# Second MLP product of a decoder block: eight pairs of row blocks summed in PSUM, pair by pair for all four banks, weight sums and additions on VectorE

## The chip, the cores and the metric

One Trainium2 chip, of which the kernel uses one core. The metric is the device time of the program in microseconds (us), the median of several runs. The profile's times are those of one execution. PE is TensorE, DVE VectorE, ACT ScalarE, POOL GpSimd, SP SyncE, whose queue issues nearly all DMAs.

## What is computed

A decoder block for 1024 tokens of width 1024: sparse attention, sliding-window attention, gates, then an MLP of width 4096, all in float32. The change touches only the last product of the MLP and the norm behind it:

```python
h2 = rmsnorm(x, mlp_norm_w)
u = relu(h2 @ w_up)                  # [1024, 4096]
x = x + (u * u) @ w_down             # [1024, 4096] @ [4096, 1024]
return rmsnorm(x, final_norm_w)
```

## The kernel before

Float32 precision comes from splitting: `split` (line 99) makes of a 128x512 block `a` a high part `h` (a rounded copy, ScalarE, line 102) and a rest `l = a - h` (VectorE, line 107). One block product is then three matmuls, h by h, h by l and l by h (lines 1103 to 1105), each 128 by 128 weights against 512 columns.

The second product is done with Strassen's scheme (Winograd's form) of seven products in place of eight. The 32 row blocks of `w_down` (128 rows of 1024 columns) form 16 pairs; a pair has four blocks of 128x512, b11, b12 (first row block, left and right half), b21, b22. Products "1" to "7" multiply operands of the activations, which the stage before has stored ready-made in `u_d[n-1, p]`, by operands of the weights, which are b11, b21, b22 or sums of blocks. Four sums for each pair are made by `sums` (lines 1080 to 1087) on GpSimd (`"pppp"`), into four tiles `dt` of their own; the last sum equals b21 minus the second.

The loop goes over chunks of `CH = 4` pairs, and in each chunk over the products in the order 1, 2, 6, 5, 7, 3, 4 (`items`, 28 of them). For each product it takes the four token blocks `j` in turn; `chain` (line 1099) sums the four pairs of the chunk into the PSUM bank of that `j`, 12 matmuls, and the bank is then read: for products 1 and 6 by `later` (ScalarE scales it into a tile `ds`, line 1236, GpSimd adds that to the sum `x3`, line 1238), for the others by `add` (one VectorE instruction, line 1232, in the trace `x<-pdx` or `x<-pdy`). Products 1, 6, 7, 4 go on in the same four banks (group x, tiles `pdx`), 2, 5, 3 in four others (group y, `pdy`); the groups change banks from chunk to chunk.

`operands` (line 1217) loads and splits the operands of a whole product, 4 of activations (`da`, split into `dao`) and 4 of weights (`dr` or `dt`, split into `dbo`), and is called one product ahead. `dao` and `dbo` have 7 buffers each, `da` has 6, `dr` 20, `dt` 12. In the first chunk the loads are issued behind the stores of the stage before (`issue_after(stored[-2])`).

In the last chunk `norm` (line 1242) follows the additions: squares on ScalarE, a product with `gf` on GpSimd or VectorE, the scaling, and the store to `out`. The very last bank is worked in two halves of 256 columns (`pdl`).

The order of the instructions on each engine is not the order of the text: a planner simulates the program and places what is ready by its slack, and it gives the tiles their addresses by their lifetimes; a tile with `bufs=N` has at most N copies alive. Each engine then runs its list in that fixed order, and the queue of SP as well.

Of the kernel before, what the change touches and what calls it, by code (L numbers as in the profile page):

```python
# [18 lines left out]
P = 128  # L19
# [73 lines left out]
def decoder_block(tc, I, out):  # L93
# [1095 lines left out]
    wd, ops = {}, {}  # L1189

    def block(c, p, i, a):

        t = dn.tile([P, H], F32, tag="dr", name="dr", bufs=20)
        with tc.issue_after(stored[-2]) if c == 0 else nullcontext():
            nc.sync.dma_start(t, I["w_down"][2 * p + i][:, a * H:(a + 1) * H])
        return t

    def weights_down(c, which):
        for p in range(c * CH, c * CH + CH):
            if 0 in which:  # L1200
                wd[p] = {"1": block(c, p, 0, 0)}
            if 1 in which:
                wd[p]["2"] = block(c, p, 1, 0)
        for p in range(c * CH, c * CH + CH):
            if 2 in which:
                b12, wd[p]["3"] = block(c, p, 0, 1), block(c, p, 1, 1)
                t = [dn.tile([P, H], F32, tag="dt", name="dt", bufs=12) for _ in range(4)]
                sums(wd[p]["1"], b12, wd[p]["2"], wd[p]["3"], t, "pppp", True)
                wd[p].update({"4": t[3], "5": t[0], "6": t[1], "7": t[2]})
# [7 lines left out]
    def operands(c, n):  # L1217
        if c == 0 and n in "126":
            weights_down(c, {"1": (0,), "2": (1,), "6": (2,)}[n])
        elif n == "1":  # L1220
            weights_down(c, (0, 1, 2))
        for p in range(c * CH, c * CH + CH):
            a = dn.tile([P, H], F32, tag="da", name="da", bufs=6)
            with tc.issue_after(stored[-2]) if c == 0 else nullcontext():
                loads["u"] = nc.sync.dma_start(a, u_d[int(n) - 1, p]).ins
            ops[n, p] = operand(dn, a, "act", "dve", "dao", 7), operand(dn, wd[p][n], "act", "dve", "dbo", 7)
        if c == 0 and n in "1657":
            residual(*{"1": (0, 0), "6": (1, 0), "5": (1, 1), "7": (0, 1)}[n])

    def add(b, o, ps):  # L1230
        cs = slice(o * H, o * H + ps.shape[-1]) if not isinstance(o, slice) else o
        nc.vector.scalar_tensor_tensor(x3[b][:, cs], ps, r2[:, b:b + 1], x3[b][:, cs], op0=ALU.mult, op1=ALU.add)

    def later(b, o, ps):
        t = dn.tile([P, H], F32, tag="ds", name="ds", bufs=6)
        nc.scalar.activation(t, ps, AF.Copy, scale=r2[:, b:b + 1])  # L1236
        cs = slice(o * H, (o + 1) * H)
        nc.gpsimd.tensor_tensor(x3[b][:, cs], x3[b][:, cs], t, ALU.add)  # L1238

    outs = {}  # L1240

# [26 lines left out]
            nc.sync.dma_start(out[bs, cs], y[:, cs])  # L1268

    held_banks = {}  # L1270
    operands(*items[0])
    for i, (c, n) in enumerate(items):
        if i + 1 < len(items):
            operands(*items[i + 1])
        if i == 7:
            with tc.issue_after(loads["u"]):
                nc.sync.dma_start(gf, I["final_norm_w"].broadcast_to([P, D]))
        end = c == NP // CH - 1
        for j in range(4):
            first = n in "125"  # L1280
            group = ("x" if n in "1674" else "y") if c % 2 == 0 else ("y" if n in "1674" else "x")
            if first:
                held_banks[group, j] = bank(DOWN[group][j], [P, H], f"pd{group}")
            ps = held_banks[group, j]
            hi, lo = 4 + j, j
            js = slice(j * P, (j + 1) * P)
            get = lambda k, s: ops[n, c * CH + k][s]

            def product():
                chain(ps, lambda k: tuple(t[:, js] for t in get(k, 0)), lambda k: get(k, 1), first, CH)  # L1290
            last = end and n == "4" and j == 3
            if last:
                parts = [slice(H, D), slice(0, 256), slice(256, H)]
                for q in (1, 2):
                    at = parts[q]
                    ps = bank(("mm", "pt")[q % 2], [P, 256], "pdl")
                    chain(ps, lambda k: tuple(t[:, js] for t in get(k, 0)), lambda k: get(k, 1), True, CH, at)
                    add(hi, at, ps)
                    norm(hi, parts, q)
                continue  # L1300
            product()
            if n == "1":
                later(lo, 0, ps)
            elif n == "2":
                add(lo, 0, ps)
                if end:
                    norm(lo, [slice(0, H), slice(H, D)], 0)
            elif n == "6":
                later(lo, 1, ps)
            elif n == "5":  # L1310
                add(hi, 1, ps)
            elif n == "7":
                add(hi, 1, ps)
                if end and j == 3:
                    add(hi, 0, ps)
                if end:
                    norm(hi, [slice(H, D), slice(0, 256), slice(256, H)] if j == 3 else [slice(H, D), slice(0, H)], 0)
            elif n == "3":
                add(lo, 1, ps)
                if end:  # L1320
                    norm(lo, [slice(0, H), slice(H, D)], 1)
            else:
                add(hi, 0, ps)
                if end:
                    norm(hi, [slice(H, D), slice(0, H)], 1)

    for es in (dn_es, _p, _r, _d, _c):
        es.close()
# [68 lines left out]
```

## Time and profile before

| | |
|---|---|
| median of 3 runs | 1485.68 us (1485.06 to 1489.48) |
| the profiled execution, its own time | 1482.99 us |
| its span in the trace | 1481.1 us |
| PE, share of the span busy | 93% |
| DVE / ACT / POOL | 78% / 53% / 44% |
| granted TensorE clock, mean | 0.981 |
| second product, first matmul to last | 1150.02 to 1473.77 us |

The page gives busy times of engines, the span in 40 slices, the chain of work that ended last, and the costliest groups of instructions. A matmul of 512 columns is shown with 0.39 us, but matmuls are pipelined, so their pace is read from one start to the next. The PE row is therefore not a measure of lost time in a stretch; the count of matmuls in it is.

### The profile page before, as it was taken

Reading aid. Unit: us, or ns where it says so; the run is one execution under the profiler, and the core shown is the slowest. Engines: PE = TensorE matmul, PEld = TensorE weight load, DVE = VectorE, ACT = ScalarE, POOL = GpSimd, SP = SyncE. Lnnn points to the kernel's source line nnn. Section 1 sums busy time; section 2 is a strip of 40 time slices with the busy share of each in tenths; the row PEclk is TensorE's granted clock in tenths of the full one; section 3 lists DMA queues with packets and bytes.
Section 4 is the critical chain, followed back from the end, with each engine's and each line's share of the span. In section 5 each row is a group of like instructions: output and inputs, shape, how many; then the busy total and the mean of one; then the engine's idle time right before and its main releaser. Section 6 shows DMA issues by size and latency. Waiting matters only on the chain.

```text
span 1481.1 us, 21434 instructions
## 1 busy us (share of the span) xinstructions
PE 1383.5 (93%) x7084; PEld 1167.8 (79%) x7084; DVE 1150.0 (78%) x2067; ACT 787.6 (53%) x1638; POOL 657.2 (44%) x573
## 2 busy tenths in 40 slices
PE   7999997888888999987999999999999889999998
PEld 6989886677788888865878788888887768787886
DVE  8666899999988974879864676556653897979797
ACT  6335436666675475943355585555554444444455
POOL 5373865664647653589716300000000873728151
PEclk9999998999999999999999999999999999999999
DMA  8321331332322121476666364444444955453333
GB/s 266 105 76 43 87 103 50 87 82 65 81 69 66 43 58 44 121 242 213 199 180 183 115 247 160 153 147 151 157 143 154 394 197 163 132 185 95 101 101 121
DMA packets 136400, 199.26 MB, mean 135 GB/s; under 512 B 16096, under 2 KB 59232, under 8 KB 136160
## 3 DMA queue, kind: packets, MB, share of 16 engines
q1 hardware_dynamic: 136144, 197.88, 42.3%
q8 instruction: 56, 0.92, 0.3%
q14 instruction: 56, 0.46, 0.1%
q10 hardware_dynamic: 144, 0.00, 0.0%
HBM read 135.18 MB, written 55.84 MB: 129 GB/s over the span
## 4 chain that ended last, share of the span: by engine, by line
PE 52%; DVE 27%; issue 6%; DMA 6%; POOL 5%; ACT 3%; SPq 0%; DVEq 0%; ACTq 0%; POOLq 0%
DVE of_a L673 7%; PE pu L1103 7%; PE pu L1105 7%; PE pu L1104 7%; DVE dbo L107 2%; PE pdx L1105 2%; PE pdy L1104 2%; PE pdy L1105 2%; PE pdy L1103 2%; PE pdx L1104 2%; DVE wide L850 2%; PE pdx L1103 2%; PE pso L113 2%; PE pso L112 2%; PE pso L111 2%
## 5 line engine op out<-in xcount | busy, mean ns | idle before, releaser
L1083 POOL TENSOR_TENSOR dt<-dr 128x512 f32<-128x512 f32 x16 | 28.9, 1805 | 302.7 <-DMA x<-x_d 302.7
L107 DVE TENSOR_TENSOR dao<-da,dao 128x512 fp32r<-128x512 f32 x112 | 113.6, 1021 | 22.8 <-ACT dao L102 22.8
L102 ACT ACTIVATE dao<-da 128x512 fp32r<-128x512 f32 x112 | 68.6, 620 | 103.3 <-PE pdx L1105 59.2
L111 PE MATMUL mm<-of_h,of_w 128*128 128x256 f32 x416 | 121.1, 292 | 0.0
L113 PE MATMUL mm<-of_h,of_w 128*128 128x256 f32 x416 | 120.5, 291 | 0.0
L112 PE MATMUL mm<-of_h,of_w 128*128 128x256 f32 x416 | 120.3, 290 | 0.0
L853 ACT ACTIVATE wide<-wide,of_a 128x257 f32<-128x257 f32 (+9 forms) x128 | 81.0, 634 | 65.6 <-DVE of_a L850 64.8
L673 DVE TENSOR_SCALAR_CACHE_REDUCE of_a<-wide,of_a 128x768 bf16<-128x768 bf16 (+5 forms) x93 | 106.0, 1140 | 0.9
L1103 PE MATMUL pu<-XT,uo 128*128 128x512 f32 x256 | 100.0, 390 | 2.4 <-DVE u L1147 1.7
L1238 POOL TENSOR_TENSOR x<-x,ds 128x512 f32<-128x512 f32 x32 | 49.3, 1556 | 113.5 <-ACT ds L1236 113.5
L1104 PE MATMUL pu<-XT,uo 128*128 128x512 f32 x256 | 99.7, 389 | 0.0
L1105 PE MATMUL pu<-XT,uo 128*128 128x512 f32 x256 | 99.4, 389 | 0.0
L111 PE MATMUL gt<-of_h 128*128 128x512 f32 x224 | 91.2, 407 | 6.9 <-ACT of_h L333 6.9
L113 PE MATMUL gt<-of_h 128*128 128x512 f32 x224 | 91.5, 409 | 2.6 <-POOL of_h L107 2.6
L675 ACT ACTIVATE of_a<-uall,of_a 128x384 int8<-128x384 f32 (+2 forms) x93 | 66.8, 718 | 50.7 <-DVE of_a L741 30.7
L834 PE MATMUL S<-of_w 128*128 128x256 f32 (+3 forms) x320 | 79.2, 339 | 14.3 <-DVE of_a L850 14.2
L112 PE MATMUL gt<-of_h 128*128 128x512 f32 x224 | 90.8, 406 | 1.0 <-DVE of_h L334 1.0
L1105 PE MATMUL pdx<-dbo,dao 128*128 128x512 f32 x224 | 87.1, 397 | 4.6 <-DVE dao L107 4.6
L1104 PE MATMUL pdx<-dbo,dao 128*128 128x512 f32 x224 | 88.1, 396 | 2.8 <-DVE dbo L107 2.1
L1103 PE MATMUL pdx<-dbo,dao 128*128 128x512 f32 x224 | 84.4, 393 | 3.9 <-ACT dbo L102 3.9
L1104 PE MATMUL pdy<-dbo,dao 128*128 128x512 f32 x220 | 85.3, 390 | 1.1 <-DVE dbo L107 1.1
L876 PE MATMUL pt<-kept,wide 128*128 128x128 f32 x408 | 68.9, 277 | 16.8 <-DVE wide L865 7.2
(288 smaller groups left out, 4598.9 us busy)
## 6 DMA issues: line engine op xcount, KB each, us to landing
u_d<-u SPq DMA_DIRECT2D x112, 256.0 KB, 2.2
da<-u_d SPq DMA_DIRECT2D x112, 256.0 KB, 3.0
ur<-in_w_up_dram SPq DMA_DIRECT2D x32, 512.0 KB, 4.7
dr<-in_w_down_dram SPq DMA_DIRECT2D x64, 256.0 KB, 5.0
z_d<-of_g SPq DMA_DIRECT2D x32, 256.0 KB, 2.2
uall<-z_d SPq DMA_DIRECT2D x32, 256.0 KB, 3.2
raw<-in_w_out_dram SPq DMA_DIRECT2D x32, 256.0 KB, 4.3
of_g<-in_w_g_dram SPq DMA_DIRECT2D x28, 256.0 KB, 2.8
```

What stands on the lines that cost most here:

```text
L102: nc.scalar.activation(h, src, AF.Copy)
L107: (nc.gpsimd if l_on == "pool" else nc.vector).tensor_tensor(l, src, f(h), ALU.subtract)
L111: ins = nc.tensor.matmul(ps, lhsT=ah, rhs=bh, start=first, stop=False)
L112: nc.tensor.matmul(ps, lhsT=ah, rhs=bl, start=False, stop=False)
L113: nc.tensor.matmul(ps, lhsT=al, rhs=bh, start=False, stop=last)
L673: nc.vector.tensor_scalar(j, src, c, None, op0=ALU.is_lt, op1=ALU.add, accum_out=a)
L834: marks["S"] = nc.tensor.matmul(pS[:, :e - c], lhsT=st.unit(b, j), rhs=kT[:, a, k0 + c:k0 + e], start=a == 0, stop=a == 1).ins
L853: nc.scalar.activation(pe, pe, AF.Exp, bias=last, scale=-1.0, accum_out=st.sm[:, j:j + 1])
L876: nc.tensor.transpose(pt[:, k, j], prob[j0 + j][:, (a + k) * P:(a + k + 1) * P], ident)
L1103: nc.tensor.matmul(ps, lhsT=ah, rhs=xh[:, at], start=f0, stop=False, skip_group_check=True)
L1104: nc.tensor.matmul(ps, lhsT=ah, rhs=xl[:, at], start=False, stop=False, skip_group_check=True)
L1105: nc.tensor.matmul(ps, lhsT=al, rhs=xh[:, at], start=False, stop=last, skip_group_check=True)
```

## The change

The chunk has 8 pairs in place of 4, so there are two chunks and 14 products of 8 pairs. The loop now goes over `flow`, steps of (chunk, product, pair): at each step the pair's operands go through the four banks, three matmuls each, and after the last pair of a product the four banks are read one behind the other. Reading is always `add` on VectorE; `later` is gone. The weights' sums are one VectorE instruction at a step of products 2, 6, 5 and 7, three of them in place into the tiles of the blocks, one into a tile `dt` of 2 buffers; GpSimd's `sums` are gone from this stage. Loads are called 6 steps ahead and operands 4 steps ahead; `dao` and `dbo` have 9 buffers each, `dr` 32. The last product of the last chunk is done bank by bank, as before, with 8 pairs.

```diff
-    CH = 4
+    CH = 8
-    items = [(c, n) for c in range(NP // CH) for n in "1265734"]
+    flow = [(c, n, p) for c in range(NP // CH) for n in "1265734" for p in range(c * CH, c * CH + CH)]
+    def block(c, p, at):
+        wd[p, at] = dn.tile([P, H], F32, tag="dr", name="dr", bufs=32)
         with tc.issue_after(stored[-2]) if c == 0 else nullcontext():
+            nc.sync.dma_start(wd[p, at], I["w_down"][2 * p + at // 2][:, at % 2 * H:(at % 2 + 1) * H])
+    def load(c, n, p):
+        if n == "1":
+            block(c, p, 0)
+        elif n == "2":
+            for at in (1, 2, 3):
+                block(c, p, at)
+        a = da[n, p] = dn.tile([P, H], F32, tag="da", name="da", bufs=6)
+        with tc.issue_after(stored[-2]) if c == 0 else nullcontext():
+            loads["u"] = nc.sync.dma_start(a, u_d[int(n) - 1, p]).ins
...
-                sums(wd[p]["1"], b12, wd[p]["2"], wd[p]["3"], t, "pppp", True)
...
+    def operands(c, n, p):
+        b11, b12, b21, b22 = (wd.get((p, at)) for at in range(4))
+        src = {"1": b11, "2": b21, "6": b11, "5": None, "7": b12, "3": b22, "4": b21}[n]
+        if n == "2":
+            nc.vector.tensor_tensor(b12, b22, b12, ALU.subtract)
+        elif n == "6":
+            nc.vector.tensor_tensor(b11, b12, b11, ALU.add)
+        elif n == "5":
+            src = dn.tile([P, H], F32, tag="dt", name="dt", bufs=2)
+            nc.vector.tensor_tensor(src, b22, b11, ALU.subtract)
+        elif n == "7":
+            nc.vector.tensor_tensor(b21, b21, b11, ALU.subtract)
+        ops[n, p] = operand(dn, da[n, p], "act", "dve", "dao", 9), operand(dn, src, "act", "dve", "dbo", 9)
...
-    def later(b, o, ps):
-        t = dn.tile([P, H], F32, tag="ds", name="ds", bufs=6)
-        nc.scalar.activation(t, ps, AF.Copy, scale=r2[:, b:b + 1])
-        nc.gpsimd.tensor_tensor(x3[b][:, cs], x3[b][:, cs], t, ALU.add)
...
+    def products(c, n, p, j, ps=None, first=False, at=slice(None)):
+        (ah, al), x = ops[n, p]
+        js = slice(j * P, (j + 1) * P)
...
+        end = p % CH == CH - 1
+        nc.tensor.matmul(ps, lhsT=ah[:, js], rhs=x[0][:, at], start=first, stop=False, skip_group_check=True)
+        nc.tensor.matmul(ps, lhsT=ah[:, js], rhs=x[1][:, at], start=False, stop=False, skip_group_check=True)
+        nc.tensor.matmul(ps, lhsT=al[:, js], rhs=x[0][:, at], start=False, stop=end, skip_group_check=True)
+    LOAD, LEAD = 6, 4
...
+    for i, (c, n, p) in enumerate(flow):
+        end = c == NP // CH - 1
+        if i + LOAD < len(flow):
+            load(*flow[i + LOAD])
+        if i + LEAD < len(flow):
+            operands(*flow[i + LEAD])
...
+        if end and n == "4":
+            continue
         for j in range(4):
+            products(c, n, p, j)
+        if p % CH == CH - 1:
+            for j in range(4):
+                done(c, n, j)
```

## Rows read from the trace of the kernel before

**Rows 1.** The page, its first line and part 1: busy us, share, instructions
```profile
span 1481.1 us, 21434 instructions
PE 1383.5 (93%) x7084; PEld 1167.8 (79%) x7084; DVE 1150.0 (78%) x2067; ACT 787.6 (53%) x1638; POOL 657.2 (44%) x573
```

**Rows 2.** Stretches: length, busy us (x instructions) by engine, clock, DMA share, GB/s
```profile
1150.00:1160.00 10.00, 10.00 (x44) 8.05 (x43) 8.51 (x14) 7.09 (x15) 5.74 (x3) 1.00 1.05 395
...
1180.00:1190.00 10.00, 6.89 (x23) 5.04 (x22) 6.84 (x8) 4.80 (x9) 7.61 (x6) 0.83 1.05 387
...
1210.00:1220.00 10.00, 6.42 (x21) 5.24 (x22) 10.00 (x11) 3.86 (x8) 6.26 (x5) 0.83 0.52 161
...
1230.00:1240.00 10.00, 10.00 (x46) 8.26 (x44) 6.84 (x12) 3.40 (x8) 0.00 (x0) 1.00 0.72 234
...
1150.00:1473.90 323.90, 311.55 (x1357) 254.53 (x1355) 278.07 (x328) 152.68 (x294) 165.97 (x104) 0.99 0.49 161
```

**Rows 3.** Waits of PE from 1150 us on: for whom, total us, times, longest
```profile
PE pdx L1105 <- DVE dao L107: 4.6, 2, 4.1
PE pdx L1103 <- ACT dbo L102: 3.9, 2, 2.7
```

**Rows 4.** Timeline of PE around its longest wait: start us, us, operation, idle before
```profile
1213.58 1.65 PE L1105 MATMUL pdx<-dbo,dao 128*128 128x512 f32 x3 [4.08 <-DVE dao L107]
1215.03 0.63 PE L1104 MATMUL pdx<-dbo,dao 128*128 128x512 f32 x1
1215.45 0.63 PE L1105 MATMUL pdx<-dbo,dao 128*128 128x512 f32 x1
```

**Rows 5.** Timeline of PE: the stage's first matmul, 12 without a wait, its last
```profile
1150.02 0.40 PE L1103 MATMUL pdx<-dbo,dao 128*128 128x512 f32 x1
...
1440.10 0.39 PE L1103 MATMUL pdx<-dbo,dao 128*128 128x512 f32 x1
...
1440.78 0.39 PE L1103 MATMUL pdy<-dbo,dao 128*128 128x512 f32 x1
...
1442.82 0.39 PE L1103 MATMUL pdy<-dbo,dao 128*128 128x512 f32 x1
...
1473.77 0.28 PE L1105 MATMUL pdl<-dbo,dao 128*128 128x256 f32 x1
```

**Rows 6.** Groups from 1149 us on, shapes apart: count, busy us, mean ns, idle before
```profile
L107 DVE TENSOR_TENSOR dao<-da,dao 128x512 fp32r<-128x512 f32 x112 | 113.6, 1021 | 22.8 <-ACT dao L102 22.8
L107 DVE TENSOR_TENSOR dbo<-dt,dbo 128x512 fp32r<-128x512 f32 x64 | 77.4, 1217 | 3.5 <-ACT dbo L102 3.3
L1238 POOL TENSOR_TENSOR x<-x,ds 128x512 f32<-128x512 f32 x32 | 49.3, 1556 | 113.5 <-ACT ds L1236 113.5
L107 DVE TENSOR_TENSOR dbo<-dr,dbo 128x512 fp32r<-128x512 f32 x44 | 37.0, 845 | 1.5 <-ACT dbo L102 1.5
L1083 POOL TENSOR_TENSOR dt<-dr 128x512 f32<-128x512 f32 x16 | 28.9, 1805 | 302.7 <-DMA x<-x_d 302.7
L1232 DVE SCALAR_TENSOR_TENSOR x<-pdx,kept,x 128x512 f32<-128x512 f32 x40 | 28.4, 740 | 7.3 <-PE pdx L1105 7.3
```

**Rows 7.** Timeline of DVE and POOL: with POOL at rest, and with POOL at work
```profile
1151.86 0.68 DVE L1089 TENSOR_TENSOR u<-u 128x512 f32<-128x512 f32 x1
1152.46 0.68 DVE L1090 TENSOR_TENSOR u<-u 128x512 f32<-128x512 f32 x1
...
1195.70 3.48 DVE L107 TENSOR_TENSOR dao<-da,dao 128x512 fp32r<-128x512 f32 x2
1196.88 1.74 POOL L1083 TENSOR_TENSOR dt<-dr 128x512 f32<-128x512 f32 x1
...
1455.59 0.68 DVE L107 TENSOR_TENSOR dbo<-dt,dbo 128x512 fp32r<-128x512 f32 x1
1456.19 0.68 DVE L107 TENSOR_TENSOR dao<-da,dao 128x512 fp32r<-128x512 f32 x1
```

**Rows 8.** Timeline of ACT at the hand-over: it reads the stage before's last bank
```profile
1152.00 0.57 ACT L1141 ACTIVATE u<-pu 128x512 f32<-128x512 f32 x1
```

More of the change, by code (lines that the diff above doesn't have):

```diff
@@ L1184, in decoder_block @@
     dn, dn_es = pools.open("dn")
-    CH = 4
+    CH = 8
     x3 = [dn.tile([P, D], F32, name=f"x3_{b}") for b in range(NB)]
     gf = dn.tile([P, D], F32, name="gf")
-    items = [(c, n) for c in range(NP // CH) for n in "1265734"]
-    wd, ops = {}, {}
-    def block(c, p, i, a):
-        t = dn.tile([P, H], F32, tag="dr", name="dr", bufs=20)
+    flow = [(c, n, p) for c in range(NP // CH) for n in "1265734" for p in range(c * CH, c * CH + CH)]
+    wd, da, ops = {}, {}, {}
+    def block(c, p, at):
+        wd[p, at] = dn.tile([P, H], F32, tag="dr", name="dr", bufs=32)
         with tc.issue_after(stored[-2]) if c == 0 else nullcontext():
[L1195 to L1207, printed above, removed]
-                sums(wd[p]["1"], b12, wd[p]["2"], wd[p]["3"], t, "pppp", True)
-                wd[p].update({"4": t[3], "5": t[0], "6": t[1], "7": t[2]})
+            nc.sync.dma_start(wd[p, at], I["w_down"][2 * p + at // 2][:, at % 2 * H:(at % 2 + 1) * H])
[8 more added lines that the diff above has]
+            loads["u"] = nc.sync.dma_start(a, u_d[int(n) - 1, p]).ins
     def residual(o, h):
@@ L1215, in residual @@
                 nc.sync.dma_start(x3[b][:, o * H:(o + 1) * H], x2_d[b, :, o * H:(o + 1) * H])
[L1217 to L1228, printed above, removed]
+    def operands(c, n, p):
[11 more added lines that the diff above has]
+        ops[n, p] = operand(dn, da[n, p], "act", "dve", "dao", 9), operand(dn, src, "act", "dve", "dbo", 9)
     def add(b, o, ps):
@@ L1232, in add @@
         nc.vector.scalar_tensor_tensor(x3[b][:, cs], ps, r2[:, b:b + 1], x3[b][:, cs], op0=ALU.mult, op1=ALU.add)
-    def later(b, o, ps):
-        t = dn.tile([P, H], F32, tag="ds", name="ds", bufs=6)
-        nc.scalar.activation(t, ps, AF.Copy, scale=r2[:, b:b + 1])
-        cs = slice(o * H, (o + 1) * H)
-        nc.gpsimd.tensor_tensor(x3[b][:, cs], x3[b][:, cs], t, ALU.add)
     outs = {}
@@ L1270, in decoder_block, with done @@
     held_banks = {}
[L1271 to L1275, printed above, removed]
+    def done(c, n, j):
+        ps, hi, lo, end = held_banks["xy"[n in "253"], j], 4 + j, j, c == NP // CH - 1
+        if n in "12":
+            add(lo, 0, ps)
+            if end and n == "2":
+                norm(lo, [slice(0, H), slice(H, D)], 0)
+        elif n == "6":
+            add(lo, 1, ps)
+        elif n == "5":
+            add(hi, 1, ps)
+        elif n == "7":
+            add(hi, 1, ps)
+            if end:
+                if j == 3:
+                    add(hi, 0, ps)
+                norm(hi, [slice(H, D), slice(0, 256), slice(256, H)] if j == 3 else [slice(H, D), slice(0, H)], 0)
+        elif n == "3":
+            add(lo, 1, ps)
+            if end:
+                norm(lo, [slice(0, H), slice(H, D)], 1)
+        else:
+            add(hi, 0, ps)
+            if end:
+                norm(hi, [slice(H, D), slice(0, H)], 1)
@@ new lines, in products @@
+    def products(c, n, p, j, ps=None, first=False, at=slice(None)):
+        (ah, al), x = ops[n, p]
+        js = slice(j * P, (j + 1) * P)
+        if ps is None:
+            group = "xy"[n in "253"]
+            if p % CH == 0 and n in "125":
+                held_banks[group, j] = bank(DOWN[group if c % 2 == 0 else "yx"[group == "y"]][j], [P, H], f"pd{group}")
+            ps, first = held_banks[group, j], p % CH == 0 and n in "125"
+        end = p % CH == CH - 1
+        nc.tensor.matmul(ps, lhsT=ah[:, js], rhs=x[0][:, at], start=first, stop=False, skip_group_check=True)
+        nc.tensor.matmul(ps, lhsT=ah[:, js], rhs=x[1][:, at], start=False, stop=False, skip_group_check=True)
+        nc.tensor.matmul(ps, lhsT=al[:, js], rhs=x[0][:, at], start=False, stop=end, skip_group_check=True)
@@ new lines, in decoder_block @@
+    LOAD, LEAD = 6, 4
+    for k in range(LOAD):
+        load(*flow[k])
+    for k in range(LEAD):
+        operands(*flow[k])
+    for i, (c, n, p) in enumerate(flow):
[4 more added lines that the diff above has]
+            operands(*flow[i + LEAD])
+        if c == 0 and p == 2 and n in "1657":
+            residual(*{"1": (0, 0), "6": (1, 0), "5": (1, 1), "7": (0, 1)}[n])
+        if c == 1 and n == "1" and p % CH == 0:
@@ L1276, in decoder_block @@
             with tc.issue_after(loads["u"]):
                 nc.sync.dma_start(gf, I["final_norm_w"].broadcast_to([P, D]))
-        end = c == NP // CH - 1
+        if end and n == "4":
+            continue
         for j in range(4):
[L1280 to L1325, printed above, removed]
@@ new lines, in decoder_block @@
+            products(c, n, p, j)
+        if p % CH == CH - 1:
+            for j in range(4):
+                done(c, n, j)
+    pairs = range(NP - CH, NP)
+    for j in range(3):
+        for p in pairs:
+            products(NP // CH - 1, "4", p, j)
+        done(NP // CH - 1, "4", j)
+    parts = [slice(H, D), slice(0, 256), slice(256, H)]
+    for q in (1, 2):
+        ps = bank(("mm", "pt")[q % 2], [P, 256], "pdl")
+        for p in pairs:
+            products(NP // CH - 1, "4", p, 3, ps, p % CH == 0, parts[q])
+        add(7, parts[q], ps)
+        norm(7, parts, q)
```

## The prediction

> **What bounds the kernel now.** I read the page first: PE is busy for 93% of the span [rows 1], so a gain has to come from matmuls that don't run, run slower, or wait. The diff changes no number of matmuls, so I went to the stage itself and asked how long it would take if PE never waited. The timeline gives the pace: 12 matmuls without a wait go from 1440.10 to 1442.82, 2.72 us, 0.2267 us each, and a change of bank among them (1440.78) costs nothing visible [rows 5]. The stage has 28 products x 4 token blocks x 4 pairs x 3 = 1344 matmuls; 12 of them are done as 24 of 256 columns, which in the timeline start 0.12 us apart. 1332 x 0.2267 + 24 x 0.12 = 304.8 us. It takes from 1150.02 to 1473.77 plus that last one's 0.12, 323.9 us [rows 5]. So **19.1 us** are lost in it, and no change of waits there can give more.
>
> Where they are lost is read from the table of stretches. A full 10 us hold 46 matmuls (those cut by the edges counted); 1180 to 1190 holds 23 and 1210 to 1220 holds 21 [rows 2]. Of the 32 stretches from 1150 to 1470 seven hold fewer than 42; together they are 83 short, 83 x 0.2267 = 18.8 us. So nearly all of the loss sits in seven places. In each of them POOL is at work and DVE full or waiting for POOL's sums; where POOL rests, as in 1230 to 1240, PE has its 46 [rows 2]. The waits name operands: DVE's rest `dao` and ACT's copy `dbo` [rows 3]; the copy came late because ACT itself waited for a sum of POOL's. Behind the longest wait the matmuls start 0.42 us apart, the lower clock, before the clock comes back [rows 4]; that is in the count.
>
> Why is VectorE late? Its subtraction of two 128x512 blocks takes 0.68 us and starts every 0.60 us when POOL rests; with POOL adding blocks at the same time two of them take 3.48 us, 1.74 each [rows 7]. Over the stage the three groups of it cost 1021, 1217 and 845 ns in the mean [rows 6]. That it isn't the transfers that slow it is seen at 1151.86: 0.60 us apart, with the DMA engines saturated [rows 2, 7]. And before the change little stands ready: with 7 buffers and 4 pairs to a product, the fourth operand of the next product can only be made when the last token block of the running one has let go of its first, some 4 us before PE wants it. Two subtractions at 1.74 us, a copy and an evacuation eat that.
>
> **The change, part by part.**
>
> *POOL's 64 sums and 32 additions go.* Four groups of 16 sums like the one shown, and 49.3 us of additions [rows 6]: POOL has nothing left in the stage but the norms' 8 instructions. The gain is not POOL's time but VectorE's: 220 subtractions at 228.0 us fall to 220 x 0.68 = 150 us of busy time, 78 us less. ScalarE loses 32 evacuations.
>
> *VectorE gets 64 sums and loses 24 evacuations.* 64 x 0.68 = +43.5 us; 80 evacuations of whole banks become 56, -24 x 0.74 = -17.8 us [rows 6, 7]. Its busy time goes from 278 [rows 2] to about 278 - 78 + 43.5 - 17.8 = 226 us of some 307. The fullest kind of product is 2, 6, 5 or 7: 8 pairs x 3 instructions x 0.60 + 4 evacuations x 0.67 (two of them take 1.41 us in the timeline) = 17.1 us, against 8 x 2.72 = 21.8 us of PE. So VectorE stays 20% under PE even there, and none of this lies on the path. Its cover is the lead below; without it a product's end would show 4 x 0.67 = 2.7 us, 14 times.
>
> *One pair at a time for all banks.* A step is 12 matmuls, 2.72 us, and needs two operands; before, the first 2.72 us of a product needed eight. With 9 buffers and operands called 4 steps ahead, 4 x 2.72 = 10.9 us stand between VectorE and PE. At a product's end VectorE waits in its list for the last matmul and then reads four banks, 2.7 us; behind these four are the operands of the fifth step on, and they have 8 us left. I cost this at nothing. The banks are wanted again only 8 steps later. The 8 norm instructions of POOL still slow VectorE in the last chunk, about 8 x 1 us, under the same cover.
>
> *Moves of PSUM banks.* There are 444 changes of bank in place of 112. The nearest row is the change at 1440.78, at the usual pace [rows 5]: 0 us, and at most 0.01 us each by the reading, so 0 to 3 us; I take 0.
>
> *The first step.* The four banks of group x are now wanted within 2.1 us of the start, at 1150.02, 1150.70, 1151.38 and 1152.06; two of them carry the tag of the stage before's accumulators. Before, ScalarE read the last of those from 1152.00 to 1152.57 [rows 8], which nobody minded. If that place in ScalarE's list stays, PE waits up to 2.6 us; if the planner moves it up to the end of the product, 0. I take 1.0.
>
> *Loads.* In the second product a step brings three blocks and one operand, 4 x 0.262 MB in 2.72 us, 386 GB/s, as much as the DMA engines move when full (387 to 395 [rows 2]). But a load is called 6 steps ahead of a step whose operands are made 4 ahead: 10 x 2.72 = 27 us in hand. The first sixteen steps need 32 blocks and 16 operands, 12.6 MB, and with 7 late stores and 4 residual blocks 15.5 MB; at 387 GB/s 40 us, from 1139.6 (the first load in the trace, which the stores fix) to 1180, and PE wants the sixteenth at 1191. Cost 0, 0 to 3 us.
>
> *What is next late.* PE itself. Matmuls run at 0.234 us in part of the first stretch (44 in place of 46 [rows 2]); this I leave in, 1.0 us, and 0.6 for small waits (0 to 3).
>
> **The sum.** The stage: 1320 x 0.2267 + 48 x 0.12 (the last bank's halves now have 24 each) = 305.0, + 1.0 + 1.0 + 0.6 = 307.6 us, against 323.9: **-16.3 us**. What comes behind the last matmul (1473.9 to 1481.1) and the stages ahead stay. The profiled execution's own time of 1482.99 becomes 1466.7; the median of the runs shown is 2.7 above that execution, so 1469.4 in the median. With all costs zero it is 1466.7, with all at their upper ends (3 + 2.6 + 3 + 1 + 3 = 12.6 in place of 2.6) 1479.4.
>
> **Rivals.**
>
> *Half the gain.* The planner's list, not POOL, holds the operands back: an evacuation or a norm stands before an operand that PE needs first. For it: lists are fixed, and VectorE in order. Against: 4 steps of lead. Price: half of the 14 product ends at 1 us each, 7 us: 1476.5.
>
> *No change to be told.* The losses of 1170 to 1220 come from the saturated DMA engines and not from POOL. For it: 1180 to 1190 has a DMA share of 1.05. Against: 1210 to 1220 has 0.52 and loses more, and 1150 to 1160 has 1.05 and loses nothing to speak of [rows 2]. These four stretches are 62 short (two are shown), 14 us, which would stay: 1483. A measurement of this kernel tells about 0.3% (4.5 us) from no change.
>
> *Slower: VectorE becomes the bound.* In the 8 products with three instructions a step, 24 x t + 2.7 us have to fit into 21.8; they do up to t = 0.80 us. To lose back the 16.3 us, 2.0 for each of the 8, t must be 0.88 us. At the pace with POOL, 1.74, the stage would be 180 us longer. For it: 1.74 us is what the trace shows much of the time. Against: each such row has POOL beside it, and POOL is gone. Were something that stays the cause, at t = 0.95 the time would be 1469.4 + 8 x 3.7 = 1499.
>
> *Slower: the clock falls by the rotation.* A matmul costs 0.2 us more at the lower clock (0.42 against 0.2267 [rows 4, 5]), so 80 matmuls at it, 6% of the stage, undo the gain; 200 give 1509. Here that would need PE to pause at the changes of bank, and the row at 1440.78 has no pause. The Trainium skill ("TensorE: Matmul & The Clock Gate", section "A second HAM failure mode: psum-queue depth-cycling") speaks against this change: it says that going round the PSUM banks leaves short idle times between groups of matmuls, in which the clock goes down and up. The trace of before, with a change every 12 matmuls, doesn't show that; one every 3 it can't show.
>
> **Chances.** Forecast 0.79, half 0.09, no change 0.05, VectorE as the bound 0.03, clock 0.04. Faster by over 0.3% is the first two, 0.88; same 0.05; slower 0.07. The range: from 1464, since the 2.7 between profile and median may be absent, to 1479, which takes in the costs' upper ends and the second case.
>
> **What would show it.** POOL at 0 in every stretch from 1160 to about 1400; the subtractions at 0.68 us in the mean; 46 matmuls in each 10 us; first matmul at about 1150, last at 1457; PE's waits in the stage under 3 us. Wrong if subtractions stay above 0.8 us, if PE waits for `dbo` at product ends or for DMAs in the second product, if the granted clock is below 1.00 in the stage, or if the stage starts later than 1150.

## The result, and the profile after

The changed kernel takes **1464.11 us** in the median of 4 runs (1461.0 to 1466.59), the kernel before 1485.37 in the same comparison (1483.75 to 1489.48). The ratio is 0.9853 with an interval of 0.9840 to 0.9866: 21.8 us less on the median shown, 1463.8. The forecast was 1469.4 with a range from 1464.0; the direction and the mechanism hold, the gain is 5.6 us larger than forecast and lies 0.2 us beyond the range's end.

The page's first line and busy times, which answer to [rows 1]:

```profile
span 1464.8 us, 21275 instructions
PE 1379.3 (94%) x7096; PEld 1169.0 (80%) x7096; DVE 1102.1 (75%) x2107; ACT 775.4 (53%) x1606; POOL 499.0 (34%) x477
```

The span fell from 1481.1 to 1464.8, by 16.3 us. That is the forecast to the tenth, and it is a trap: the two profiled executions didn't start the changed part at the same time. The timeline of PE, changed kernel: the first matmul of the first MLP product, the hand-over between the two products, and the last matmul.

```profile
845.26 0.50 PE L1103 MATMUL pu<-X,uo 128*128 128x512 f32 x1 [0.19 <-ACT uo L102]
...
1149.71 0.39 PE L1105 MATMUL pu<-XT,uo 128*128 128x512 f32 x1
1149.94 0.39 PE L1300 MATMUL pdx<-dbo,dao 128*128 128x512 f32 x1
...
1152.67 0.40 PE L1103 MATMUL pu<-XT,uo 128*128 128x512 f32 x1
...
1155.40 0.86 PE L1301 MATMUL pdx<-dbo,dao 128*128 128x512 f32 x3
...
1457.89 0.28 PE L1302 MATMUL pdl<-dbo,dao 128*128 128x256 f32 x1
```

And the same places of the kernel before (its last two products are in [rows 5]):

```profile
840.61 0.50 PE L1103 MATMUL pu<-X,uo 128*128 128x512 f32 x1
...
1145.09 0.39 PE L1105 MATMUL pu<-XT,uo 128*128 128x512 f32 x1
1147.12 0.50 PE L1103 MATMUL pu<-XT,uo 128*128 128x512 f32 x1 [1.65 <-DVE u L1147]
```

Up to the hand-over the lists of instructions of both kernels are the same on every engine, yet this first matmul comes at 840.61 in one and at 845.26 in the other; over all kernels of this study it came between 839.6 and 845.3. So the span compares executions, not kernels. The measure that follows is the stretch **from the first matmul of the first MLP product to the last of the second**: 1473.77 - 840.61 = 633.16 us before, 1457.89 - 845.26 = 612.63 after, **20.5 us less**. The ratio of the medians says 21.8 (19.9 to 23.8), so the stretch holds the gain within that interval. Three kernels whose matmuls and operands are those of the changed one (it, e6 and e10 below) have 612.6, 612.5 and 613.0; differences above 1 us are read as real.

The fence also shows the two parts of the gain. In the changed kernel PE does 12 matmuls of the second product (1149.94 to 1152.67), goes back to the first for its last 12, and takes up the second at 1155.40. The second product therefore takes 12 x 0.2267 = 2.7 us, and from 1155.40 to 1457.89 + 0.12, 302.6: **305.3 us against 323.9**, 18.5 less. The first product takes the rest, 307.4 against the 309.4 from 840.61 to 1150.02: **2.0 less**. Before, PE stood 1.65 us idle at 1147.12 ahead of the last 12 matmuls of the first product, until VectorE had read the bank in which they go on (`u<-pu`); now 12 matmuls of the second product fill that gap.

The table of stretches, columns as in [rows 2], same stretches:

```profile
1150.00:1160.00 10.00, 10.00 (x45) 8.20 (x44) 9.30 (x16) 9.74 (x19) 0.00 (x0) 1.00 1.05 390
1180.00:1190.00 10.00, 10.00 (x46) 8.29 (x45) 7.35 (x12) 2.46 (x5) 0.00 (x0) 1.00 1.02 376
1210.00:1220.00 10.00, 10.00 (x46) 8.27 (x45) 10.00 (x17) 6.59 (x12) 0.00 (x0) 1.00 0.88 309
...
1149.90:1457.20 307.30, 307.30 (x1375) 254.91 (x1375) 233.03 (x377) 146.23 (x271) 10.45 (x8) 1.00 0.54 180
```

The stretches that had 23 and 21 matmuls have 46, at DMA shares of 1.02 and 0.88, and the granted clock is 1.00. POOL has 8 instructions left. PE has no wait at all from 1150 us on, where [rows 3] showed 4.6 and 3.9 us. VectorE has 233.0 us of work in place of 278.1. Its groups, which answer to [rows 6] (columns: line, engine, operation, output<-input, shape, count | busy us, mean ns | idle before and what ended it):

```profile
L107 DVE TENSOR_TENSOR dao<-da,dao 128x512 fp32r<-128x512 f32 x112 | 76.0, 685 | 38.5 <-ACT dao L102 38.2
L107 DVE TENSOR_TENSOR dbo<-dr,dbo 128x512 fp32r<-128x512 f32 x96 | 66.2, 695 | 3.2 <-ACT dbo L102 3.2
L1231 DVE SCALAR_TENSOR_TENSOR x<-pdx,kept,x 128x512 f32<-128x512 f32 x32 | 23.0, 744 | 11.3 <-PE pdx L1302 11.3
L1221 DVE TENSOR_TENSOR dr<-dr 128x512 f32<-128x512 f32 x16 | 11.0, 686 | 0.2
```

The subtractions fell from 1021, 1217 and 845 ns to 685 and 695; the weight sums, now VectorE's, take 686 ns in the group shown, where POOL took 1805 in its [rows 6].

### The profile page after: what moved, and what is told of

The parts are those of the page before. It is cut to its first block, busy times and chain, and to the rows that moved or that the text cites. A ratio compares the mean times of both kernels' runs of the same rounds, so it can differ in the third digit from the quotient of the medians.

```text
span 1464.8 us, 21275 instructions
## 1 busy us (share of the span) xinstructions
PE 1379.3 (94%) x7096; PEld 1169.0 (80%) x7096; DVE 1102.1 (75%) x2107; ACT 775.4 (53%) x1606; POOL 499.0 (34%) x477
## 4 chain that ended last, share of the span: by engine, by line
PE 64%; DVE 22%; issue 4%; DMA 4%; ACT 3%; POOL 2%; SPq 1%; DVEq 0%; ACTq 0%; POOLq 0%
PE pu L1103 7%; PE pu L1105 7%; PE pu L1104 7%; DVE of_a L673 6%; PE pdx L1302 4%; PE pdx L1300 4%; PE pdx L1301 4%; PE pdy L1300 3%; PE pdy L1302 3%; PE pdy L1301 3%; DVE wide L850 2%; PE pso L113 2%; PE pso L112 2%; PE pso L111 2%; PE S L834 2%
## 5 line engine op out<-in xcount | busy, mean ns | idle before, releaser
L1247 POOL TENSOR_TENSOR y<-x,gf 128x512 f32<-128x512 f32 x4 | 6.4, 1616 | 492.8 <-DVE x L1231 492.8
L107 DVE TENSOR_TENSOR dao<-da,dao 128x512 fp32r<-128x512 f32 x112 | 76.0, 685 | 38.5 <-ACT dao L102 38.2
L1301 PE MATMUL pdx<-dbo,dao 128*128 128x512 f32 x248 | 95.0, 390 | 0.0
L1300 PE MATMUL pdx<-dbo,dao 128*128 128x512 f32 x248 | 94.8, 389 | 0.0
L1302 PE MATMUL pdx<-dbo,dao 128*128 128x512 f32 x248 | 92.9, 390 | 0.0
L111 PEld LDWEIGHTS mm<-of_h,of_w 128*128 128x128 f32 x416 | 82.7, 199 | 0.8
L113 PEld LDWEIGHTS mm<-of_h,of_w 128*128 128x128 f32 x416 | 82.2, 198 | 1.4 <-POOL of_w L107 0.3
```

The costliest lines, as they stand in the source:

```text
L111: ins = nc.tensor.matmul(ps, lhsT=ah, rhs=bh, start=first, stop=False)
L113: nc.tensor.matmul(ps, lhsT=al, rhs=bh, start=False, stop=last)
L1300: nc.tensor.matmul(ps, lhsT=ah[:, js], rhs=x[0][:, at], start=first, stop=False, skip_group_check=True)
L1301: nc.tensor.matmul(ps, lhsT=ah[:, js], rhs=x[1][:, at], start=False, stop=False, skip_group_check=True)
L1302: nc.tensor.matmul(ps, lhsT=al[:, js], rhs=x[0][:, at], start=False, stop=end, skip_group_check=True)
```

## The experiments

**The theory** is that POOL's additions slow VectorE's two-operand instructions, that the operands then come late, and that nothing else was lost in the stage. **Rivals**: the new loop and the deeper buffers bring the gain and POOL's absence is a by-product; POOL's sums are themselves late (a chain of data, not contention); the hand-over brings part. Three kernels (e2 to e4) edit the one before, nine the changed one; the stretch is read from one execution of each; ratios are against runs of the kernel before on the same chip.

| kernel | stretch, us | median, us | ratio (interval) |
|---|---|---|---|
| before | 633.16 | 1485.37 | |
| changed | 612.63 | 1464.11 | 0.9853 (0.9840 to 0.9866) |
| e1: sums on POOL | 620.65 | 1470.94 | 0.9918 (0.9902 to 0.9935) |
| e2: before, sums on VectorE | 621.15 | 1469.05 | 0.9903 (0.9885 to 0.9921) |
| e3: before, POOL without work | 614.75 | 1463.52 | 0.9867 (0.9852 to 0.9882) |
| e4: before, 9 buffers | 628.47 | 1478.32 | 0.9961 (0.9950 to 0.9973) |
| e5: unconnected POOL additions | 623.05 | 1472.35 | 0.9916 (0.9893 to 0.9939) |
| e6: unconnected POOL fills | 612.54 | 1465.22 | 0.9869 (0.9851 to 0.9888) |
| e7: chunks of 4 pairs | 616.09 | 1466.86 | 0.9888 (0.9864 to 0.9911) |
| e8: hand-over as before | 615.76 | 1465.50 | 0.9869 (0.9846 to 0.9891) |
| e9: 3 buffers, 2 steps ahead | 616.83 | 1465.51 | 0.9871 (0.9851 to 0.9891) |
| e10: POOL fills beside VectorE | 612.96 | 1461.88 | 0.9849 (0.9830 to 0.9869) |
| e11: 64 more VectorE additions | 617.82 | 1467.87 | 0.9894 (0.9873 to 0.9914) |
| e12: 128 more | 634.77 | 1483.66 | 0.9995 (0.9985 to 1.0004) |

### Which part of the change pays

**e1: the changed kernel with its 64 sums back on POOL.**

```diff
-            nc.vector.tensor_tensor(b12, b22, b12, ALU.subtract)
+            nc.gpsimd.tensor_tensor(b12, b22, b12, ALU.subtract)
...
```

(the same for the other three sums)

> The changed kernel with its 64 sums of weight blocks given back to GpSimd, in place as they are. Theory A (GpSimd's work beside VectorE is what made operands late): the subtractions next to it go back to 1.7 us, the 64 sums are 64 x 1.74 = 111 us of GpSimd, and PE waits again in products 2, 6, 5 and 7; between a third and all of the gain is lost, 1470 to 1485 us. Rival B (the lead of four steps and the pairwise order made the gain): the subtractions may be slow, but PE doesn't see it; 1463 to 1466 us, no wait of PE over 1 us in the stage.

Measured: 8.0 us more in the stretch than the changed kernel. The loss sits in one place, 1187 to 1203, products 2 and 6 of the first chunk. PE's one wait there (for whom: total us, times, longest), and the table of stretches there and in the second chunk:

```profile
PE pdy L1301 <- DVE dbo L107: 4.5, 1, 4.5
```

```profile
1190.00:1200.00 10.00, 5.54 (x18) 4.14 (x17) 10.00 (x7) 6.84 (x13) 10.00 (x7) 0.79 0.63 191
1290.00:1370.00 80.00, 80.00 (x354) 66.27 (x353) 68.73 (x73) 37.12 (x68) 46.89 (x29) 1.00 0.32 99
```

Seven VectorE instructions fill 10 us beside seven of POOL, 1.4 us each. So in the first chunk the new loop with all its lead doesn't carry POOL's sums. In the second it does: POOL is at work for 46.9 of 80 us, and PE has its full count (80 / 0.2267 = 353). A slowed VectorE costs time only where PE catches up with it. Nor does the sum of POOL's work tell the price: with the same 64 sums on POOL the loss is 8.0 us here and 12.0 in the old loop (next).

**e2: the kernel before, the 64 sums on VectorE**, POOL's 32 additions of `later` kept.

```diff
-                sums(wd[p]["1"], b12, wd[p]["2"], wd[p]["3"], t, "pppp", True)
+                sums(wd[p]["1"], b12, wd[p]["2"], wd[p]["3"], t, "dddd", True)
```

> The kernel before with nothing changed but the engine of its 64 sums, VectorE in place of GpSimd; the 32 additions stay on GpSimd. Theory A: the subtractions fall towards 0.7 us and most of the gain is there without the new loop, 1466 to 1472 us. Rival B: the product ends still come too early for the operands, 1478 us or more.

Measured: 12.0 us of the stretch gone by one word, though VectorE got 64 instructions more. What is left is again a meeting with POOL, this time with additions of which no operand depends. Timeline of VectorE and POOL (start us, us, engine, operation):

```profile
1183.65 8.48 POOL L1238 TENSOR_TENSOR x<-x,ds 128x512 f32<-128x512 f32 x4 [18.38 <-ACT ds L1236]
1185.23 0.68 DVE L1083 TENSOR_TENSOR dt<-dr 128x512 f32<-128x512 f32 x1
1185.94 1.68 DVE L1084 TENSOR_TENSOR dt<-dr,dt 128x512 f32<-128x512 f32 x1
1187.54 1.77 DVE L1085 TENSOR_TENSOR dt<-dr 128x512 f32<-128x512 f32 x1
1189.24 1.78 DVE L1086 TENSOR_TENSOR dt<-dr,dt 128x512 f32<-128x512 f32 x1
...
1193.21 0.68 DVE L107 TENSOR_TENSOR dao<-da,dao 128x512 fp32r<-128x512 f32 x1
```

VectorE's sum takes 1.68 to 1.78 us beside POOL's four additions and 0.68 behind them; POOL's take 8.48 us together. The row at 1185.23 is still at 0.68: the first of POOL's additions takes 3.42 us from 1183.65 on, twice as long as the others, while VectorE keeps its pace. In the waits PE then has 3.4 us for a `dao` of VectorE.

**e3: e2, and the additions of products 1 and 6 on VectorE too.** POOL keeps the norms' instructions; loop, chunks of 4 pairs and 7 buffers stay as before.

```diff
-                later(lo, 0, ps)
+                add(lo, 0, ps)
...
-                later(lo, 1, ps)
+                add(lo, 1, ps)
```

> The kernel before with the sums on VectorE and products 1 and 6 added by VectorE too, so that GpSimd has only the norms; loop, chunks and buffers as before. Theory A: subtractions at 0.68 us, 1465 to 1470 us, and what is left to the changed kernel (0 to 5 us) is the worth of the new loop. Rival B: 1475 us or more, with waits of PE at the ends of products.

Measured: another 6.4 us gone, 1463.52 in the median, which can't be told from the changed kernel. In the stretches that had 23 and 21 matmuls it has 46, and PE's only wait is that of the hand-over:

```profile
1180.00:1190.00 10.00, 10.00 (x46) 8.29 (x45) 10.00 (x18) 4.72 (x9) 0.00 (x0) 1.00 1.05 383
1210.00:1220.00 10.00, 10.00 (x46) 8.29 (x45) 10.00 (x18) 3.55 (x7) 0.00 (x0) 1.00 0.49 142
```

```profile
PE pu L1103 <- DVE u L1147: 1.6, 1, 1.6
```

The gain thus comes apart as 12.0 us (POOL's sums) + 6.4 (POOL's additions) + 2.1 (e3 to the changed kernel) = 20.5. Eight pairs, the turn through the banks, 9 buffers and the longer lead are not needed for the first two.

**e4: the kernel before with 9 buffers for `dao` and `dbo`**, POOL working as before.

```diff
-            ops[n, p] = operand(dn, a, "act", "dve", "dao", 7), operand(dn, wd[p][n], "act", "dve", "dbo", 7)
+            ops[n, p] = operand(dn, a, "act", "dve", "dao", 9), operand(dn, wd[p][n], "act", "dve", "dbo", 9)
```

> The kernel before with 9 buffers in place of 7 for the split operands, GpSimd's work as before. Theory A: GpSimd still slows VectorE and its sums still come late, 1478 to 1485 us. Rival B: the deeper lead alone gives most of the gain, 1465 to 1472 us.

Measured: 4.7 us less in the stretch, 0.39% in the median of 10 runs. Deeper buffers cover a quarter of what POOL costs and don't touch its cause: the `dao` subtractions keep a mean of 1045 ns (1021 in [rows 6]), and PE still waits (view of the waits):

```profile
PE pdx L1103 <- ACT dbo L102: 4.2, 2, 2.7
PE pdx L1105 <- DVE dao L107: 3.5, 3, 1.9
```

### Contention or a chain of data

**e5: the changed kernel with 64 additions on POOL whose results nobody reads**; `da` and the loads' lead go from 6 to 5 to make room for the tile.

```diff
+        if n in "2657":
+            idle = dn.tile([P, H], F32, tag="ds", name="ds", bufs=1)
+            nc.gpsimd.tensor_tensor(idle, da[n, p], da[n, p], ALU.add)
```

> The changed kernel with 64 additions on GpSimd that nobody waits for (a loaded block of 128x512 doubled into a tile of its own, at each step of products 2, 6, 5 and 7); da has 5 buffers and loads are called 5 steps ahead, since the tile needs the room. Theory A (the two engines hold each other up when both read two blocks): VectorE's subtractions are slowed from 0.69 to 0.85-1.1 us in the mean, GpSimd's take 1.7 us, though no data goes between them; PE waits little because of the lead, 1464 to 1471 us. Rival B (operands were late because GpSimd's sums were late as data, not because VectorE was slowed): subtractions stay at 0.69 us and the time at 1464.

Measured: 10.4 us more in the stretch, and in the median somewhat more than expected, since PE did wait (6.1 us in three waits). All of it lies between 1182 and 1206, where VectorE is busy for 23.8 of 24 us. The smaller `da` and the shorter lead of the loads can account for a part of it at most: e8 has them too and is 3.1 us longer in all, its hand-over included. The groups give POOL's additions 104.2 us, 1644 ns each, and the `dao` subtractions 795 in the mean, 685 in the changed kernel. Timeline, where POOL stops within the fence:

```profile
1174.92 1.52 DVE L1219 TENSOR_TENSOR dr<-dr 128x512 f32<-128x512 f32 x1
1175.86 4.38 POOL L1229 TENSOR_TENSOR ds<-da 128x512 f32<-128x512 f32 x3
1176.37 1.52 DVE L107 TENSOR_TENSOR dao<-da,dao 128x512 fp32r<-128x512 f32 x1
1177.81 1.52 DVE L1221 TENSOR_TENSOR dr<-dr 128x512 f32<-128x512 f32 x1
1179.26 1.52 DVE L107 TENSOR_TENSOR dao<-da,dao 128x512 fp32r<-128x512 f32 x1
1180.71 0.68 DVE L1226 TENSOR_TENSOR dr<-dr 128x512 f32<-128x512 f32 x1
1181.31 0.68 DVE L107 TENSOR_TENSOR dao<-da,dao 128x512 fp32r<-128x512 f32 x1
```

Beside POOL the starts lie 1.45 us apart, and 0.60 as soon as POOL is through. No instruction of VectorE waits for these additions, so a chain of data is out as the cause of its slowing: the engines stand in each other's way.

**e6: in the same place a fill of an own tile by POOL** (`nc.gpsimd.memset(idle, 0.0)`, two buffers, nobody reads it).

> The changed kernel with 64 instructions on GpSimd that only write a block of 128x512 (zeros) and read none, at the same places. Theory A, with the read of two blocks as what is shared: VectorE's subtractions stay at 0.69 us and the time at 1464 us. Rival: any work of GpSimd in SBUF slows VectorE: 0.8 us or more in the mean.

Measured: nothing lost, 612.5 us, but this run doesn't tell: with no reader to hold them, all 64 fills ran in POOL's free time between 0.9 and 57.7 us, beside none of the stage's work.

**e10: the fills tied to their place**, 192 of them, written into `da` once its operand is made, so that they come between the stage's own instructions.

```diff
         ops[n, p] = operand(dn, da[n, p], "act", "dve", "dao", 9), operand(dn, src, "act", "dve", "dbo", 9)
+        if n in "2657":
+            for _ in range(3):
+                nc.gpsimd.memset(da[n, p], 0.0)
```

> The changed kernel with 192 zero fills of 128x512 on GpSimd (0.53 us each, 100 us, as much as the additions beside it were), three at each step of products 2, 6, 5 and 7, into the loaded operand after it has been split: they write and read nothing. In the earlier run of this kind the fills went to the start of the program, since nothing held them back. Theory: what is shared is the read of two blocks, so the subtractions stay at 0.69 us and the time at 1464 to 1466 us. Rival: any work of GpSimd in the memory slows VectorE, 0.8 us or more in the mean.

Measured: 0.3 us more in the stretch with 98.0 us of POOL, about as much of its time as the 104.2 of e5. Groups, and the timeline where they overlap:

```profile
L1230 POOL MEMSET da<- 128x512 f32 x192 | 98.0, 527 | 432.4 <-DMA da<-u_d 309.5 <-DVE dao L107 117.7
L107 DVE TENSOR_TENSOR dao<-da,dao 128x512 fp32r<-128x512 f32 x112 | 76.6, 690 | 34.9 <-ACT dao L102 34.6
```

```profile
1306.62 3.34 POOL L1230 MEMSET da<- 128x512 f32 x6 [64.39 <-DVE dao L107]
1307.07 0.69 DVE L107 TENSOR_TENSOR dao<-da,dao 128x512 fp32r<-128x512 f32 x1
1307.67 0.69 DVE L107 TENSOR_TENSOR dbo<-dr,dbo 128x512 fp32r<-128x512 f32 x1
1308.27 1.29 DVE L1226 TENSOR_TENSOR dr<-dr 128x512 f32<-128x512 f32 x2
```

The subtractions run at their 0.60-us pace in the midst of POOL's writes. So it isn't any work of POOL that slows VectorE: what the additions do and the fills don't is read blocks. That it matters whether VectorE reads two is seen in its additions of whole banks to `x` (`x<-pdx` and `x<-pdy`), which read one block and one PSUM bank: in the trace of before the 19 that lie wholly beside POOL's work took 738 ns in the mean, the 58 beside none of it 742. The Trainium skill ("SBUF — State Buffer", section "Who interferes with whom") says this: an instruction of VectorE with two inputs in SBUF contends with one of GpSimd that reads SBUF, not with one that only writes it. Both halves agree with e5 (0.60 to 1.45 us) and e10 (0.60 stays).

### What the new loop is worth

**e7: the changed kernel with chunks of 4 pairs** (`CH = 8` becomes 4).

> The changed kernel with chunks of 4 pairs in place of 8: 112 reads of banks on VectorE in place of 56, 41 us more of its work, spread. Theory: PE is what bounds the stage and VectorE has room (233 of 307 us busy), so no change, 1463 to 1467 us, PE without waits in the stage. Rival (eight pairs in a sum are what freed VectorE): 1470 us or more.

Measured: 3.5 us more in the stretch; the ratio's interval overlaps that of the changed kernel, so the medians don't settle it. PE's waits come to 1.2 us for a `dao` of ScalarE and 0.4 for one of VectorE, both between 1172 and 1189. The timeline has the rest as well: after a gap the first matmul takes 0.34 us to the next start in place of 0.227, and with the gaps behind 1144.06, 1172.69, 1174.11, 1183.90 and 1187.26 this makes 3.2 us over the pace. From 1190 to 1450 PE is at its full pace. So eight pairs are worth 3.5 us, all ahead of 1190, where VectorE is busy without a break from 1160 on.

**e8: the 12 matmuls of the first pair held behind the last of the first product**, with `da` and the loads' lead at 5 as in e5.

```diff
-        product(b1, "4", False)
+        marks["up"] = product(b1, "4", False)
...
-            products(c, n, p, j)
+            with tc.issue_after(marks["up"]) if i == 0 else nullcontext():
+                products(c, n, p, j)
```

> The changed kernel with the first pair's 12 matmuls held behind the last matmul of the stage before (order only, on PE); da has 5 buffers and loads are called 5 steps ahead, so that the tiles find room. Theory: PE again waits 1.6 us ahead of the last product of the stage before, starts it at the lower clock, and the stretch from that stage's first matmul to the last of all is about 2 us longer than in the changed kernel (612.5 us), 614.5; in the time that is 0.14%, about as much as can be told. Rival: the wait only moves, same stretch within 0.5 us.

Measured: 3.1 us more in the stretch. The hand-over's wait is back, and one of about its size later, which the fifth `da` buffer may explain (view of the waits):

```profile
PE pu L1103 <- DVE u L1148: 1.2, 1, 1.2
PE pdy L1303 <- DVE dao L107: 1.1, 1, 1.1
```

With e3, which has the old hand-over and 2.1 us more than the changed kernel, this makes the hand-over the place of the last 2 us. It is read from stretches of single executions; in the medians two such microseconds don't show.

**e9: 3 buffers and operands called 2 steps ahead** in place of 9 and 4 (the last five pairs, which are worked bank by bank, keep their own five).

```diff
+        tail = c == NP // CH - 1 and n == "4" and p % CH > 2
+        x, y, m = ("daz", "dbz", 5) if tail else ("dao", "dbo", 3)
...
-    LOAD, LEAD = 6, 4
+    LOAD, LEAD = 6, 2
```

> The changed kernel with 3 buffers in place of 9 for the split operands (8 again for the last product, which holds all of them), operands called 2 steps ahead. By the prediction's cover: with so little lead the reading of four banks behind each product (2.7 us) shows, at up to 14 ends, up to 38 us; I expect waits of PE at the ends of products of 5 to 30 us together, 1469 to 1495 us. Rival: three buffers are lead enough, since a step is 2.72 us and its operands take 1.8: 1464 to 1467 us.

Measured: no wait of PE at all in the stage, where 5 to 30 us were expected; 4.2 us more in the stretch, spread over gaps too small for the view of waits, and a ratio whose interval overlaps that of the changed kernel. So the operands of two steps nearly do: they are 2 x 2.72 = 5.4 us of PE, twice the 2.7 that a product's end takes on VectorE.

### How near VectorE is to being the bound

**e11 and e12: one and two more additions on VectorE in each step of products 2, 6, 5, 7**, with results that nobody reads.

```diff
+        if n in "2657":
+            idle = dn.tile([P, H], F32, tag="ds", name="ds", bufs=1)
+            for _ in range(1):
+                nc.vector.tensor_tensor(idle, da[n, p], da[n, p], ALU.add)
```

(`range(2)` in e12; `da` and the loads' lead 5 in both)

> The changed kernel with one more addition of two blocks on VectorE at each step of products 2, 6, 5 and 7 (64, into a tile of its own that nobody reads; da has 5 buffers, loads 5 steps ahead). By the prediction's sum a product then needs 8 x 4 x 0.60 + 2.7 = 21.9 us of VectorE against 21.8 of PE: just at the bound, with the lead nothing or little is lost, 1464 to 1469 us.

> The same with two more additions at each of these steps (128). A product needs 8 x 5 x 0.60 + 2.7 = 26.7 us of VectorE against 21.8: 4.9 us lost in each of 8 products, 39 us, less the lead of some 11 to 13 us ahead of each run of four such products: 1477 to 1503 us. If it stays under 1470, VectorE's bound lies further off than the prediction's sum has it.

Measured: 5.2 and 22.1 us more in the stretch; e12 has lost the whole gain. PE's waits for one operand in e11, then a late stretch of e11, then e12 in two halves (columns as in [rows 2]):

```profile
PE pdy L1306 <- DVE dao L107: 4.0, 2, 3.0
```

```profile
1200.00:1450.00 250.00, 250.00 (x1103) 206.74 (x1102) 214.17 (x349) 114.89 (x214) 10.30 (x8) 1.00 0.43 147
```

```profile
1150.00:1300.00 150.00, 136.87 (x568) 108.72 (x567) 143.59 (x234) 63.87 (x109) 0.00 (x0) 0.97 0.68 235
1300.00:1450.00 150.00, 150.00 (x661) 123.82 (x660) 146.43 (x240) 70.31 (x128) 6.30 (x4) 1.00 0.31 99
```

In these products e11 has four instructions to a step, 8 x 4 x 0.60 + 2.7 = 21.9 us against PE's 21.8; e12 has five, 26.7. If that sum decided, e12 would lose 4.9 us in each of eight products, four of them in the second chunk. But 250 us at full pace hold 1103 matmuls and 150 us hold 662: e11 loses nothing behind 1200, and e12 next to nothing behind 1300, where the same additions keep VectorE busy for 146.4 of 150 us. VectorE's instructions are spread over the products of a chunk, so the sum that fits there is the chunk's: an estimate from the same rows, with 40 instructions in each of four products, 16 in each of three, and 28 banks to read, is (4 x 40 + 3 x 16) x 0.60 + 28 x 0.67 = 143.6 us in e12, against 7 x 21.8 = 152.6 of PE. Nearly all of the loss is in the first chunk, as in e1 and e5; what makes that chunk the tight one was not tried apart. A part of e11's 5.2 us may also be due to its five `da` buffers, since e8, with the same, has a wait of 1.1 us at about the same place.

## Why the prediction was right in its cause and wrong in its size

**Right: what was lost, and why.** The ceiling of 19.1 us for the stage was read from the pace of 12 matmuls and from missing matmuls in the stretches; e2 and e3 gave 18.4 us back in the old loop by moving POOL's work to VectorE. The step from POOL to VectorE was argued from two timelines [rows 7]; e5 shows it without a link of data, and e10 that writes alone don't do it. The step that VectorE would do with more instructions less work (226 us forecast, 233.0 measured) held, as did each sign named in advance: first matmul at 1150, last at 1457, 46 matmuls in 10 us, subtractions at 0.68 us (685 and 695 ns), POOL idle but for the norms, PE's waits under 3 us. The two times among them were luck in part: this execution reached the first product 4.7 us late, and the 4.2 us that were gained beyond the forecast hid that.

**Wrong: "the stages ahead stay".** They lost 2.0 us (309.4 to 307.4). The prediction looked at the hand-over for what it may cost (a bank that ScalarE reads late, 0 to 2.6 us, taken as 1.0) and not for what it may give: the wait of 1.65 us at 1147.12 was in the trace, and a step of the new loop needs two operands where a product of the old one needed eight, so it can be ready in time to fill that gap. e8 and e3, which keep the old place, keep the wait (1.2 and 1.6 us). The missing term was one of a gain, and no end of the range had it: with all costs at nothing the sum ended at 1466.7, and the range was carried lower only by the 2.7 us between profile and median.

**Mis-sized: the costs in the stage.** 1.0 for the first step, 1.0 for the pace and 0.6 for small waits were 2.6 us together; the stage took 305.3 us against the bare 305.0, so they came to 0.3. The first step cost nothing although ScalarE reads the last bank of the stage before even later than it did, in the timeline of the changed kernel at

```profile
1157.15 0.58 ACT L1141 ACTIVATE u<-pu 128x512 f32<-128x512 f32 x1
```

The 12 matmuls that fill the gap are six of line 1300 and three each of lines 1301 and 1302: the first pair for three banks and the start of the second. By the order of the lines PE goes on with three banks until 1158.9 and then takes up the fourth. The slower pace of the first stretch is still there, but short: it holds 45 matmuls, where it held 44. The stage thus gained 18.5 us where 16.3 were forecast; these 2.2 us and the 2.0 ahead make up the 4.2 by which the stretch gained more. With the stretch alone the median would be 1485.7 - 20.5 = 1465.2, inside the range. Of the 1.3 us up to 21.8, 0.4 lie behind the last matmul (7.3 us before, 6.9 after), and the rest is less than the ratio's interval can tell; so the 4.2 us are a miss of the sum, and the last 0.2 below the range may be chance.

**More than was needed: the cover.** The prediction set a lead of four steps against the 2.7 us that each product's end takes on VectorE, 14 times, 38 us without a lead. e9 has half the lead and a third of the buffers and lost 4.2, none of it as a wait: PE works on through the operands that stand ready, and those of two steps are enough. No run was made without any lead.

**Wrong without effect.** The prediction gave the loads 10 steps, 27 us, in hand. In the loop a load is called 6 steps ahead of its matmuls and 2 ahead of its split, not 6 + 4; PE has no wait in the stage, so it cost nothing. The loop's text gives about 420 changes of bank, not 444, at a price of 0. And the weight sums do not fall into the products in whose steps they are called, so the sum of 17.1 us for one product is not what VectorE did in it (in the second chunk none of the sums of products 5 and 7 runs during them).

**The rivals.** Half the gain by the planner's order: PE has no wait, so no. No change because the DMA engines are saturated: 46 matmuls at a DMA share of 1.02 in the changed kernel and of 1.05 in e3 rule it out. VectorE as the bound: VectorE can become it, as e12 shows, but not by the rival's sum. The point where its work just fits was put at 0.80 us an instruction, which is e11's load (32 x 0.60 = 24 x 0.80), and a loss is there; but it lies in the first chunk alone, while the second carries even e12's load, so that the point agrees is luck. The clock: 1.00 in every 10 us of the stage, at 46 or 45 matmuls, with a change of bank after every third; so going round the four banks costs nothing that can be seen. The Trainium skill ("TensorE: Matmul & The Clock Gate", section "A second HAM failure mode: psum-queue depth-cycling") speaks of short idle times between groups of matmuls; here PE has none to be seen, and the trace shows no fall of the clock. It falls where PE waits, to 0.83 in the kernel before [rows 2] and to 0.79 in e1.

**Not settled**: where in each step e9 loses its 4 us; why the first chunk is the tight one; what five `da` buffers cost by themselves; and the 2.7 us of the first MLP product over its bare pace (1344 x 0.2267 = 304.7), some 2 us of which lie in its first 10 and which the change doesn't touch.

## What to carry to other kernels

Work given to GpSimd isn't free because GpSimd is idle: if it reads blocks while VectorE reads two, both can slow down, and giving VectorE more instructions can leave it less work; compare the same instruction's time with GpSimd at rest and at work before moving anything. When a stage's first step needs fewer operands than before, look at the waits of the stage ahead too: they are places that the new step can fill, and belong into the range as a gain. Compare kernels from a mark that both have, not by their spans, when unchanged stages vary by as much as the effect.

## What the runs showed of the chip that was not expected

POOL's fills, 98.0 us of them among VectorE's subtractions, cost VectorE next to nothing (690 ns against 685), while beside POOL's additions its pace went from 0.60 to 1.45 us; the slowing ends with POOL's last instruction. In e5 that slowing cost PE time only from 1182 to 1206; from 1310 to 1450 POOL was at work for 56.0 of 140 us, and PE had its 619 matmuls. Changes of bank after every third matmul cost nothing that can be seen (46 matmuls in 10 us at a granted clock of 1.00). Instructions that are the same in two kernels, up to the first MLP product, took from 839.6 to 845.3 us.
